# Moving VectorE's row sums and the adaLN gate products to other places of an attention layer

## Chip, cores and metric

The kernel runs on one core of one Trainium2 chip. The metric is the device time of one execution in microseconds (us); the median of the runs counts. TensorE is called PE, VectorE DVE, ScalarE ACT, GpSimd POOL, and SyncE, which only issues DMAs, SP.

## What is computed

A two-layer trunk: layer 0 mixes tokens by gated grouped-query attention, layer 1 by a gated linear recurrence. There are 512 latent tokens and 128 prompt tokens (640 in all), 1024 features, 16 heads of 64 and 4 key heads. Cut to what matters here:

```python
sh, sc, g = split(silu(cond) @ ada_w[i] + ada_b[i], 3)      # per layer; two conditions: latent, prompt
h = x * (1 + sc) + sh
q, k, v, gp = split(h @ attn_w_in, ...)                     # layer 0
q, k = rope(rms_norm(q)), rope(rms_norm(k))                 # the prompt tokens without rope
out = (softmax(q @ k.T / 8) @ v * silu(gp)) @ attn_w_out
x = layer_norm(alpha * x + g * out)
```

Each layer thus needs a shift `sh`, a scale `sc` and a gate `g` of 1024 numbers for each of two conditions. Layer 1 needs its shift and scale only when layer 0 is done, and a gate is needed only in the norm that ends its layer.

## The kernel before

**Products.** An fp32 product is done as three matmuls of split operands: hi times hi, lo times hi, hi times lo. A weight tile of 128x1024 comes by DMA on SP into one of three buffers (`raw`), ACT casts it to the high part (line 240) and DVE subtracts for the low part (line 241, `wlo`). The input projection `attn_w_in` has ten chunks of 256 columns: 0 to 3 are the queries of four heads each, 4 and 5 keys and values, 6 to 9 the gate path.

**The lead-in** (`lead_in`) computes the gate path, 16 half tiles of 24 matmuls (`feat_mms`, lines 349 to 351, out `gps`; ACT applies SiLU). Between them stand the query chunk 0's statistics and its later steps: the scale `rq` by POOL (line 191), normalising `qn` (615), rotary products `u` and `r` (654, 656, 658), ACT's cast (693) and DVE's `qs` (694) as a split, PE's transposes (702), ACT's copy into X (704), which frees the PSUM bank; likewise the keys (`sl`, 667; transposes 676).

**Attention.** After the lead-in the attention of four head chunks runs (`att_gen`): scores (869, 870), row maximum `nm` on DVE (964), exponential `p` on ACT (969), reciprocal `rc` on DVE (974), scaling of `p` on POOL (975), transposes (982) and copies `pts` (874) on ACT and DVE, product `pot` (896), gating into `gs` (901). Beside chunk c-1's attention runs `q_gen` for query chunk c = 1, 2, 3: "beside chunk c" here means beside that projection of query chunk c. `weave` mixes the two by a given share. `split_gs` (1106, 1107, the second on POOL) splits the gated output, and `wo_gen` prepares the output weights; the output projection follows.

**Work without a place of its own.** `q_gen` takes a filler and lets it go a step at fixed points, then drains what is left of it ahead of the last query split. There are two kinds:

- `ada_gen(layer)`: the gate of one layer, four steps of PE products over two weight tiles each (`ada_mms`, line 284, loads of `in_ada_s` on SP), each added to `acc` by DVE (321), then four stores on POOL (325). Layer 0's then loads the gate's broadcast, two DMAs on POOL's queue. It stands beside chunk 2 (layer 0) and chunk 3 (layer 1).
- `ada_cols`: shift and scale of layer 1 by row sums on DVE. Of a 128x1024 weight tile (512 KB, `in_ada_c`) and the broadcast SiLU of each condition, one DVE instruction (line 335, `scalar_tensor_tensor`) multiplies and sums along the row; its product is thrown away into a spill tile. There are 16 tiles, so 32 row sums. Twelve tiles (24 sums) are taken in the lead-in, one tile after each half tile, with two buffers (`adaraw`) loaded by `cols_load` on SP and the spill in a part of `gs` that is not yet in use. Four tiles (8 sums) are the filler `cols_gen` beside chunk 1, from the three `raw` buffers and with a spill tile of `prep` (tag `s2`, two buffers, which the key split `s` uses too).

**What sets the order.** The first half is one scheduled block: a scheduler orders each engine's instructions at build, with the code's order as its start. The order on an engine is then fixed, and an instruction that waits holds what is behind it on that engine. SP's loads keep the order of a list (lines 396 to 402).

Of the kernel before, what the change touches and what calls it, by code (L numbers as in the profile page):

```python
# [11 lines left out]
F32 = mybir.dt.float32  # L12
# [6 lines left out]
P = 128  # L19
D = 1024  # L20
# [13 lines left out]
ALPHA = 4.0 ** 0.25  # L34
HALVES = ((0, 320), (320, 640))
RAW_AHEAD = 2
LEAD = (1, 1)
RAW_START = 8
EARLY = 2
# [9 lines left out]
D_OUT = 5.5  # L49
SLIP = 1.0  # L50
COLS = [(s, ft) for s in range(2) for ft in range(KT)]
COLS_LATE = 4


def view(t, off, dims):
# [72 lines left out]
def drain(gen):  # L128
    for _ in gen:
        pass  # L130
# [3 lines left out]
def hybrid_step(ctx: ExitStack, tc: tile.TileContext, a: dict, o: dict):  # L134
# [176 lines left out]
    def gate_load(layer, eng):  # L311
        for s in range(2):
            eng.dma_start(gate[layer][:, s, :], gated[layer][s:s + 1, :].to_broadcast((P, D)))

    def ada_gen(layer):
        acc = rowp.tile([P, CW], F32, tag="row", name="acc")
        nc.gpsimd.dma_start(acc, a["ada_bias"][layer])
        for i in range(4):
            ps = bank1("adaps")
            ada_mms(ps, layer, i)  # L320
            nc.vector.tensor_tensor(acc, acc, ps[:, :CW], ALU.add)
            yield
        yield
        for q in range(4):
            nc.gpsimd.dma_start(gated[layer][:, q * CW:(q + 1) * CW], acc[32 * q:32 * q + 2, :])
        yield
        if layer == 0:
            gate[0] = gsp.tile([P, 2, D], F32, tag="gate", name="gate0")
            gate_load(0, nc.gpsimd)

    def ada_cols(job, raw, spill):

        s, ft = job
        for c in range(2):
            nc.vector.scalar_tensor_tensor(spill, raw, 1.0, silb[:, c, :], ALU.mult, ALU.mult,
                                           accum_out=shsc[1][:, s, ft, c:c + 1])
        if ft == KT - 1:
            nc.vector.tensor_tensor(shsc[1][:, s], shsc[1][:, s], view(adab, (3 + s) * KT, [[1, KT], [0, 2]]), ALU.add)

    def cols_gen():  # L340
        for job in COLS[len(COLS) - COLS_LATE:]:
            ada_cols(job, take(("ada_c",) + job), prep.tile([P, D], F32, tag="s2", name="spill", bufs=2))
            pump()
            yield

    def feat_mms(ps, w, mt, j, hhi, hlo):
        c, t = slice(mt * P, (mt + 1) * P), slice(*HALVES[j])
# [30 lines left out]
    def ada_pieces(sup):  # L378
        return [("ada_s", sup, k) for k in range(KT)]
# [16 lines left out]
        order.extend(pieces("attn_w_in", c))  # L396
    for c in range(3):
        order.extend(pieces("attn_w_in", c + 1))
        order.extend(ada_pieces(c - 1) if c else [("ada_c",) + job for job in COLS[len(COLS) - COLS_LATE:]])
    order.extend(("attn_w_out", nh, i) for nh, i in PIECES)  # L400
    order.extend(("rec_w_in", h, i) for h in range(RH) for i in range(5))
    order.extend(("rec_w_out", nh, i) for nh, i in OUT1)
# [310 lines left out]
    def q_gen(c, X, fill):  # L713

        w = Weights("attn_w_in", c, (nc.vector, nc.vector), tuple(last_split))
        yield
        if c > 1:
            next(fill)
            yield
        pend = None  # L720
        for tt0, n in UNITS:
            ps = yield from tok_unit(w, tt0, n, "qmm")
            rstd = rms_stat(ps, n)
            r = rope_raw(ps, tt0, n, cosq, sinq, qg)
            yield
            if pend:
                for i in range(pend[1]):
                    pend[0](i)
                    yield
            next(fill, None)  # L730
            yield
            yield
            qn = rms_scale(r, n, rstd)
            yield
# [18 lines left out]
    def lead_in(att):  # L753
# [88 lines left out]

        for _ in range(2):
            cols_load()
        step = 0
        for ch in range(6, 10):
            if ch < 9:
                ws[ch + 1] = Weights("attn_w_in", ch + 1, LEAD_LO)
            w = ws.pop(ch)
            for mt in range(2):  # L850
                for j, (t0, t1) in enumerate(HALVES):
                    ps = bank_any("gps")
                    feat_mms(ps, w, mt, j, hhi, hlo)
                    nc.scalar.activation(gs[:, 2 * (ch - 6) + mt, t0:t1], ps[:, :320], AF.Silu)
                    step += 1
                    if step % 2 or not later:
                        settle()
                    if step % 2 and later:
                        later.pop(0)()
                    if raws:  # L860
                        ada_cols(*raws.popleft(), gs[:, KT - 2:, :].rearrange("p a b -> p (a b)")[:, :D])
                        cols_load()
                    if step > 16 - EARLY:
                        next(att)
        assert not raws


    def score_mms(out, X, c, h, t0, k0, k1):
# [253 lines left out]

    def q_next(c):
        Xs[c] = xq[c % 2].tile([P, 4, NT], F32R, tag="X", name=f"X{c}")
        yield from q_gen(c, Xs[c], ada_gen(c - 2) if c > 1 else cols_gen())

    for c in range(1, 4):
        side.items.append((f"q{c}", q_next(c), lambda c=c: front_of[0] >= c - 1))
# [647 lines left out]
```

## Time and profile before

| | |
|---|---|
| median of 3 runs | 842.29 us (842.24 to 848.55) |
| profiled execution | 844.78 us; its span 843.0 us, mean granted PE clock 0.99 |
| busy, share of the span | PE 808.0 us (96%), DVE 559.9 (66%), ACT 386.5 (46%), POOL 215.8 (26%) |
| DMA | 93.28 MB |
| lead-in's row sums (24) | 71.6 to 122.0 us of the span |
| row sums beside chunk 1 (8) | 144.3 to 185.5 us |

In the trace's rows the first number is the start within the span, the second the duration; then come engine, line, operation, result and operands by the program's names (`out<-in`) and shapes. In brackets stand the engine's idle time ahead of the instruction and what ended it. In a list of waits, "PE x L1 <- DVE y L2: a, n, b" means that PE at line 1 waited for DVE's line 2 for a us in n waits, the longest b. A row of a table of stretches holds the length, and for PE, its weight loads, DVE, ACT and POOL busy time and number of instructions, then the granted clock, the DMA engines' busy share and GB/s. A group's row has three durations in ns: lowest, median, highest.

### The profile page before, as it was taken

The numbers are of one execution on the slowest core, as the hardware profiler recorded it, in microseconds if no ns is written. First come the engines' busy times: TensorE is split into PE (matmuls) and PEld (weight loads), VectorE is DVE, ScalarE is ACT, GpSimd is POOL, SyncE is SP. The second block draws the span as 40 slices with busy tenths as digits, with TensorE's granted clock in tenths as the row PEclk, the third lists the DMA queues.
The fourth block names the chain that finished last, engine by engine and source line by source line (L and its number), as shares of the span: only waits on it lengthen the run. The fifth ranks groups of instructions, "written<-read, shape, count | busy, mean of one in ns | idle before, by whom it ended". The sixth has DMA issues, their size and how long they took to land.

```text
span 843.0 us, 19206 instructions
## 1 busy us (share of the span) xinstructions
PE 808.0 (96%) x8025; PEld 729.2 (87%) x8025; DVE 559.9 (66%) x996; ACT 386.5 (46%) x782; POOL 215.8 (26%) x261
## 2 busy tenths in 40 slices
PE   8999899989999988999999999999999999999994
PEld 6789799878878766888999999999999999998774
DVE  4568882795657674776438575767668575858477
ACT  2252354674656776222434444435434544445232
POOL 0123001443344833010001304143333314121121
PEclk9999899999999999999999999999999999999998
DMA  9944451114151230630322322231322312324041
GB/s 325 397 145 165 151 175 52 51 54 148 51 200 51 101 100 1 225 125 35 108 69 68 103 72 82 83 109 51 107 89 83 99 61 89 120 65 157 23 161 75
DMA packets 34326, 93.28 MB, mean 111 GB/s; under 512 B 5040, under 2 KB 12224, under 8 KB 34240
## 3 DMA queue, kind: packets, MB, share of 16 engines
q1 hardware_dynamic: 23568, 74.10, 25.9%
q0 software_dynamic: 4768, 14.18, 5.4%
q10 hardware_dynamic: 5904, 3.78, 1.5%
q8 instruction: 63, 1.03, 0.5%
q14 instruction: 23, 0.19, 0.1%
HBM read 82.85 MB, written 9.19 MB: 109 GB/s over the span
## 4 chain that ended last, share of the span: by engine, by line
PE 82%; DVE 9%; ACT 2%; DMA 2%; issue 2%; POOL 1%; SPq 0%; DVEq 0%; ACTq 0%; POOLq 0%
PE rps L1319 7%; PE rps L1320 7%; PE rps L1321 7%; PE vgps L1309 5%; PE vgps L1311 5%; PE vgps L1310 5%; PE pot L896 4%; PE outp L1158 4%; PE outp L1160 3%; PE outp L1159 3%; PE pt L982 3%; PE lv L1452 2%; PE acc L536 2%; PE gps L349 2%; PE sc L869 2%
## 5 line engine op out<-in xcount | busy, mean ns | idle before, releaser
L1319 PE MATMUL rps<-h1hi,rhi 128*128 128x320 f32 x368 | 118.4, 322 | 0.0
L1320 PE MATMUL rps<-h1lo,rhi 128*128 128x320 f32 x368 | 113.9, 309 | 0.0
L1321 PE MATMUL rps<-h1hi,rlo 128*128 128x320 f32 x368 | 113.8, 309 | 0.0
L975 POOL TENSOR_SCALAR p<-p,rc 128x640 f32<-128x640 f32 x64 | 58.8, 921 | 116.6 <-DVE rc L974 102.3
L1319 PEld LDWEIGHTS rps<-h1hi,rhi 128*128 128x128 f32 x368 | 69.2, 188 | 1.3
L1320 PEld LDWEIGHTS rps<-h1lo,rhi 128*128 128x128 f32 x368 | 69.3, 188 | 0.0
L1321 PEld LDWEIGHTS rps<-h1hi,rlo 128*128 128x128 f32 x368 | 69.1, 188 | 0.0
L241 DVE TENSOR_TENSOR rlo<-raw,rhi 128x1024 fp32r<-128x1024 f32 x32 | 45.0, 1409 | 33.8 <-ACT rhi L240 33.8
L964 DVE TENSOR_REDUCE nm<-sc 128x1 f32<-128x640 f32 x64 | 52.0, 818 | 23.2 <-PE sc L870 22.8
L1480 POOL COPY At<-near 32x160 f32<-32x160 f32 x32 | 14.0, 438 | 196.8 <-DVE near L1442 195.8
L969 ACT ACTIVATE p<-sc,nm 128x640 f32<-128x640 f32 x64 | 51.2, 802 | 27.2 <-DVE nm L964 19.3
L240 ACT CAST rhi<-raw 128x1024 fp32r<-128x1024 f32 x32 | 33.6, 1049 | 52.0 <-PE rps L1320 48.8
L1430 ACT COPY kc<-A 128x640 f32<-128x640 f32 x40 | 32.2, 806 | 54.4 <-DVE A L1461 50.5
L1309 PE MATMUL vgps<-rhi,h1hi 128*128 128x256 f32 x180 | 51.5, 286 | 0.0
L1310 PE MATMUL vgps<-rlo,h1hi 128*128 128x256 f32 x180 | 50.9, 283 | 0.0
L1311 PE MATMUL vgps<-rhi,h1lo 128*128 128x256 f32 x180 | 50.9, 283 | 0.0
L982 PE MATMUL pt<-small,p 128*128 128x128 f32 x320 | 48.6, 276 | 1.4 <-ACT pts L874 0.9
L869 PE MATMUL sc<-kk,X 128*128 128x320 f32 x128 | 42.6, 343 | 6.1 <-ACT p L969 6.0
L874 ACT COPY pts<-pt 128x512 f32<-128x512 f32 x64 | 35.8, 591 | 24.4 <-PE pt L982 24.1
L982 PEld LDWEIGHTS pt<-small,p 128*128 128x128 f32 x320 | 37.1, 140 | 7.8 <-issue 5.3
L1309 PE MATMUL vgps<-wspare,h1hi 128*128 128x256 f32 x140 | 41.8, 298 | 0.0
L896 PE MATMUL pot<-pts,vv 128*64 128x256 f32 x320 | 38.9, 386 | 2.4 <-DVE pts L874 2.4
(301 smaller groups left out, 2423.6 us busy)
## 6 DMA issues: line engine op xcount, KB each, us to landing
raw<-in_rec_w_in SPq DMA_DIRECT2D x40, 512.0 KB, 3.7
raw<-in_ada_m SPq DMA_DIRECT2D x16, 512.0 KB, 8.0
raw<-in_attn_w_in SPq DMA_DIRECT2D x16, 512.0 KB, 4.2
raw<-in_ada_s SPq DMA_DIRECT2D x16, 512.0 KB, 4.4
adaraw<-in_ada_c SPq DMA_DIRECT2D x12, 512.0 KB, 3.8
raw<-in_attn_w_out SPq DMA_DIRECT2D x8, 512.0 KB, 4.1
raw<-in_rec_w_out SPq DMA_DIRECT2D x8, 512.0 KB, 3.5
x1d<-y SPq DMA_DIRECT2D x5, 512.0 KB, 2.6
```

The source lines that it names most:

```text
L869: nc.tensor.matmul(out, X[:, h, t0:t0 + P], kk[:, c, k0:k1], start=True, stop=False)
L896: nc.tensor.matmul(pot[j * HD:(j + 1) * HD, :CW], vv[:, slot, c * HD:(c + 1) * HD], moving[j], start=first, stop=last)
L964: nc.vector.tensor_reduce(nm[:, 0:1], sc[:, :, :320], AX.XY, ALU.max, negate=True)
L969: return nc.scalar.activation(halves(p[:]), sc[:, :, :320], AF.Exp, bias=nm[:, 0:1], accum_out=su[:, 0:1])
L975: nc.gpsimd.tensor_scalar(p, p, rs[:, 0:1], 1.0, ALU.mult, ALU.mult)
L982: nc.tensor.transpose(pt[:, i * 256 + q * P:i * 256 + (q + 1) * P], ps[q][:, (k0 + i) * P:(k0 + i + 1) * P], ident)
L1309: nc.tensor.matmul(out, h1hi[:, k, t], hi, start=(k == 0), stop=False)
L1310: nc.tensor.matmul(out, h1hi[:, k, t], lo, start=False, stop=False)
L1311: nc.tensor.matmul(out, h1lo[:, k, t], hi, start=False, stop=(k == KT - 1))
L1319: nc.tensor.matmul(ps[:, j, :320], hi[:, k, :], h1hi[:, k, t], start=(k == 0), stop=False)
L1320: nc.tensor.matmul(ps[:, j, :320], hi[:, k, :], h1lo[:, k, t], start=False, stop=False)
L1321: nc.tensor.matmul(ps[:, j, :320], lo[:, k, :], h1hi[:, k, t], start=False, stop=(k == KT - 1))
```

## The change

Four things are changed; the number of row sums, products, loads and stores stays.

1. The lead-in takes eleven tiles (22 row sums) in place of twelve. How many sums follow each half tile is set by the table `ROWS_AT`: none after the first four, one after the fifth and sixth, two after the seventh to the fifteenth, none after the last. Each is "issued after" the SiLU of its half tile (`issue_after` names an instruction that must have been issued before), and what is left is drained at the end.
2. The lead-in's spill tile is the part of `gs` only up to the twelfth half tile, then the `s2` tile of `prep`.
3. The fillers are exchanged: layer 0's gate stands beside chunk 1, layer 1's beside chunk 2, and five tiles (10 row sums) beside chunk 3. The loads of layer 0's gate broadcast move from the end of its products to the end of those five tiles. The list of SP's loads follows.
4. A filler's steps are at spots given by `FILL_AT` ("0b": after the first token tile of unit 0; "0e", "2e", "4e": after units 0, 2, 4), so four steps and the drain, and for row sums a step is one sum.

```diff
+FILL_AT = {1: "0b0e2e4e", 2: "0b0e2e4e", 3: "0b0e2e4e"}
-COLS_LATE = 4
+COLS_LATE = 5
+ROWS_AT = (0, 0, 0, 0, 1, 1, 2, 2, 2, 2, 2, 2, 2, 2, 2, 0)
...
     def ada_gen(layer):
...
-        if layer == 0:
-            gate[0] = gsp.tile([P, 2, D], F32, tag="gate", name="gate0")
-            gate_load(0, nc.gpsimd)
-
-    def ada_cols(job, raw, spill):
+
+    def ada_cols(job, raw, spill, after):
 
         s, ft = job
         for c in range(2):
-            nc.vector.scalar_tensor_tensor(spill, raw, 1.0, silb[:, c, :], ALU.mult, ALU.mult,
-                                           accum_out=shsc[1][:, s, ft, c:c + 1])
+            with tc.issue_after(after()) if after else ExitStack():
+                nc.vector.scalar_tensor_tensor(spill(), raw, 1.0, silb[:, c, :], ALU.mult, ALU.mult,
+                                               accum_out=shsc[1][:, s, ft, c:c + 1])
+            yield
...
+    def spare():
+        return prep.tile([P, D], F32, tag="s2", name="spill", bufs=2)
+
     def cols_gen():
         for job in COLS[len(COLS) - COLS_LATE:]:
-            ada_cols(job, take(("ada_c",) + job), prep.tile([P, D], F32, tag="s2", name="spill", bufs=2))
+            yield from ada_cols(job, take(("ada_c",) + job), spare, None)
             pump()
-            yield
+        gate[0] = gsp.tile([P, 2, D], F32, tag="gate", name="gate0")
+        gate_load(0, nc.gpsimd)
...
-        order.extend(ada_pieces(c - 1) if c else [("ada_c",) + job for job in COLS[len(COLS) - COLS_LATE:]])
+        order.extend(ada_pieces(c) if c < 2 else [("ada_c",) + job for job in COLS[len(COLS) - COLS_LATE:]])
...
-        if c > 1:
-            next(fill)
-            yield
+        spots = {FILL_AT[c][i:i + 2] for i in range(0, len(FILL_AT[c]), 2)}
...
+                if f"{tt0}{'0abcd'[step]}" in spots:
+                    next(fill, None)
+                    yield
...
-            next(fill, None)
-            yield
+            if f"{tt0}e" in spots:
+                next(fill, None)
+                yield
...
+        silus = []
+
+        def spill():
+            return gs[:, KT - 2:, :].rearrange("p a b -> p (a b)")[:, :D] if len(silus) <= 12 else spare()
+
+        def cols_steps():
+            while raws:
+                yield from ada_cols(*raws.popleft(), spill, lambda: silus[-1])
+                cols_load()
+
+        cgen = cols_steps()
...
-                    nc.scalar.activation(gs[:, 2 * (ch - 6) + mt, t0:t1], ps[:, :320], AF.Silu)
+                    silus.append(nc.scalar.activation(gs[:, 2 * (ch - 6) + mt, t0:t1], ps[:, :320], AF.Silu).ins)
...
-                    if raws:
-                        ada_cols(*raws.popleft(), gs[:, KT - 2:, :].rearrange("p a b -> p (a b)")[:, :D])
-                        cols_load()
+                    for _ in range(ROWS_AT[step - 1]):
+                        next(cgen, None)
...
-        assert not raws
+        drain(cgen)
...
-        yield from q_gen(c, Xs[c], ada_gen(c - 2) if c > 1 else cols_gen())
+        yield from q_gen(c, Xs[c], ada_gen(c - 1) if c < 3 else cols_gen())
```

The next rows show what stands on an engine in a row; line numbers shift by 2 to 27 in the changed kernel. First DVE in the lead-in, from the query statistics (190, then 192) to the first query split `qs`, before:

```order
L190 TENSOR_SCALAR rs_t<-ssq 128x20
L335 SCALAR_TENSOR_TENSOR gs,shsc_80<-adaraw,silb 128x1024 x3
L615 TENSOR_TENSOR qn<-pmm,rq 128x512
L335 SCALAR_TENSOR_TENSOR gs,shsc_80<-adaraw,silb 128x1024
L654 TENSOR_TENSOR u<-qn,sinq 128x512
L656 TENSOR_TENSOR r<-qn,cosq 128x512
L335 SCALAR_TENSOR_TENSOR gs,shsc_80<-adaraw,silb 128x1024
L658 TENSOR_TENSOR r<-r,u 128x512
L615 TENSOR_TENSOR qn<-pmm,rq 128x512
L335 SCALAR_TENSOR_TENSOR gs,shsc_80<-adaraw,silb 128x1024
L654 TENSOR_TENSOR u<-qn,sinq 128x512
L694 TENSOR_TENSOR qs_924<-r,qs_924 128x8x64
```

The same place in the changed kernel:

```order
L192 TENSOR_SCALAR rs_t<-ssq 128x20
L335 SCALAR_TENSOR_TENSOR gs,shsc_80<-adaraw,silb 128x1024 x2
L620 TENSOR_TENSOR qn<-pmm,rq 128x512
L659 TENSOR_TENSOR u<-qn,sinq 128x512
L661 TENSOR_TENSOR r<-qn,cosq 128x512
L663 TENSOR_TENSOR r<-r,u 128x512
L699 TENSOR_TENSOR qs_924<-r,qs_924 128x8x64
```

Six row sums stood between the statistics and the split; two are left, both ahead of `qn`, and two more row sums stand ahead of the statistics in both kernels. On SP the loads `adaraw` were two, then four behind the next two weight tiles of `attn_w_in`; now two come behind the next four weight tiles, and seven behind two more, ahead of the gate products' eight.

DVE at the end of the lead-in, before, up to the first row maxima `nm`; `wlo` are chunk 1's weight splits:

```order
L667 TENSOR_TENSOR sl<-kr,s_1340 128x512
L335 SCALAR_TENSOR_TENSOR gs,shsc_80<-adaraw,silb 128x1024 x5
L667 TENSOR_TENSOR sl<-kr,s_1422 128x256
L241 TENSOR_TENSOR wlo<-raw,whi 128x1024
L964 TENSOR_REDUCE nm<-sc 128x1
L241 TENSOR_TENSOR wlo<-raw,whi 128x1024
L964 TENSOR_REDUCE nm<-sc 128x1
```

And in the changed kernel:

```order
L672 TENSOR_TENSOR sl<-kr,s_1317 128x512
L335 SCALAR_TENSOR_TENSOR gs,shsc_80<-adaraw,silb 128x1024 x6
L672 TENSOR_TENSOR sl<-kr,s_1403 128x256
L243 TENSOR_TENSOR wlo<-raw,whi 128x1024
L335 SCALAR_TENSOR_TENSOR spill,shsc_80<-adaraw,silb 128x1024 x2
L339 TENSOR_TENSOR shsc_80<-shsc_80,small 128x16
L335 SCALAR_TENSOR_TENSOR spill,shsc_80<-adaraw,silb 128x1024 x6
L991 TENSOR_REDUCE nm<-sc 128x1
L243 TENSOR_TENSOR wlo<-raw,whi 128x1024
L991 TENSOR_REDUCE nm<-sc 128x1
```

Eight row sums with the `s2` spill now stand between the first weight split and the first maximum.

DVE at the end of chunk 3, before, from the last normalising `qn` through the last query split; `wolo` are the output weights:

```order
L641 TENSOR_TENSOR qn<-r,rstd 128x256
L321 TENSOR_TENSOR acc<-acc,adaps 128x256
L874 COPY pts<-pt 128x256
L964 TENSOR_REDUCE nm<-sc 128x1
L974 RECIPROCAL rc<-su 128x1
L874 COPY pts<-pt 128x256
L694 TENSOR_TENSOR qs_3552<-qn,qs_3552 128x4x64
L964 TENSOR_REDUCE nm<-sc 128x1
L974 RECIPROCAL rc<-su 128x1 x2
L241 TENSOR_TENSOR wolo<-raw,wohi 128x1024
```

And in the changed kernel:

```order
L646 TENSOR_TENSOR qn<-r,rstd 128x256
L335 SCALAR_TENSOR_TENSOR spill,shsc_80<-raw,silb 128x1024
L1001 RECIPROCAL rc<-su 128x1
L901 COPY pts<-pt 128x256
L1001 RECIPROCAL rc<-su 128x1
L991 TENSOR_REDUCE nm<-sc 128x1
L335 SCALAR_TENSOR_TENSOR spill,shsc_80<-raw,silb 128x1024
L699 TENSOR_TENSOR qs_3546<-qn,qs_3546 128x4x64
L991 TENSOR_REDUCE nm<-sc 128x1
L1001 RECIPROCAL rc<-su 128x1
L335 SCALAR_TENSOR_TENSOR spill,shsc_80<-raw,silb 128x1024
L928 TENSOR_TENSOR gs<-pot,gs 128x256
```

Row sums now stand among the row maxima, reciprocals and copies there, and POOL's four gate stores have left this place.

More of the change, by code (lines that the diff above doesn't have):

```diff
@@ L716, in q_gen @@
         yield
-        if c > 1:
-            next(fill)
-            yield
+        spots = {FILL_AT[c][i:i + 2] for i in range(0, len(FILL_AT[c]), 2)}
         pend = None
         for tt0, n in UNITS:
-            ps = yield from tok_unit(w, tt0, n, "qmm")
+            ps = None
+            gen = tok_unit(w, tt0, n, "qmm")
+            step = 0
+            while ps is None:
+                try:
+                    next(gen)
+                except StopIteration as e:
+                    ps = e.value
+                    break
+                step += 1
+                yield
+                if f"{tt0}{'0abcd'[step]}" in spots:
+                    next(fill, None)
+                    yield
             rstd = rms_stat(ps, n)
@@ L729, in q_gen @@
                     yield
-            next(fill, None)
-            yield
+            if f"{tt0}e" in spots:
+                next(fill, None)
+                yield
             yield
```

## Prediction

> **What bounds the kernel now.** I read the page's busy times first, then the chain that ended last, then TensorE's waits stage by stage.
>
> ```profile
> span 843.0 us, 19206 instructions
> PE 808.0 (96%) x8025; PEld 729.2 (87%) x8025; DVE 559.9 (66%) x996; ACT 386.5 (46%) x782; POOL 215.8 (26%) x261
> PEclk9999899999999999999999999999999999999998
> PE 82%; DVE 9%; ACT 2%; DMA 2%; issue 2%; POOL 1%; SPq 0%; DVEq 0%; ACTq 0%; POOLq 0%
> ```
>
> TensorE (PE) is busy 96% of the span and carries 82% of the chain, so an edit off PE pays only where PE waits, or runs slow. The clock digits show one dip, in the fifth slice (84 to 105 us). VectorE (DVE) is 9% of the chain: it is the one that PE waits for. The next three views are PE's waits between 82 and 142 us, stretches of that part (the columns are length, then busy time and instructions per engine, clock, DMA) and DVE just ahead.
>
> ```profile
> PE qps L702 <- DVE qs L694: 3.9, 1, 3.9
> 86.40:90.30 3.90, 0.00 (x1) 0.00 (x1) 3.90 (x9) 1.05 (x2) 0.00 (x0) 0.80 0.23 70
> 91.78:95.64 3.86, 3.86 (x15) 3.86 (x15) 3.86 (x8) 1.57 (x3) 0.00 (x0) 0.51 0.28 113
> 105.00:140.00 35.00, 35.00 (x257) 34.97 (x255) 19.22 (x30) 17.73 (x35) 0.00 (x0) 1.00 0.36 121
> ```
>
> ```profile
> 77.94 4.47 POOL L191 TENSOR_TENSOR rq<-rs_t,mhalf 128x20 f32<-128x20 f32 x1 [7.90 <-DVE rs_t L190]
> 82.45 0.69 DVE L615 TENSOR_TENSOR qn<-pmm,rq 128x512 f32<-128x512 f32 x1 [0.85 <-POOL rq L191]
> 83.06 1.21 DVE L335 SCALAR_TENSOR_TENSOR gs<-adaraw,silb 128x1024 f32<-128x1024 f32 x1
> 84.19 0.69 DVE L654 TENSOR_TENSOR u<-qn,sinq 128x512 f32<-128x512 f32 x1
> 84.80 0.69 DVE L656 TENSOR_TENSOR r<-qn,cosq 128x512 f32<-128x512 f32 x1
> ...
> 87.75 1.22 DVE L335 SCALAR_TENSOR_TENSOR gs<-adaraw,silb 128x1024 f32<-128x1024 f32 x1
> 89.49 0.69 DVE L694 TENSOR_TENSOR qs<-r,qs 128x512 fp32r<-128x512 f32 x1
> ```
>
> Reader, see this: PE stands still for 3.9 us because the first query split `qs` comes only at 89.49. Between the normalised `qn` and `qs` stand three row sums, some 1.2 us each (the first and the last of them are shown). Behind the stall the granted clock is 0.51 for 3.86 us, while the clock digits ahead of it and behind read 9. From 105 to 140 PE has no idle time, with DVE half free and POOL empty.
>
> PE's waits beside the first query chunk (142 to 192 us) and the stretches of the attention follow.
>
> ```profile
> PE sc L869 <- ACT p L969: 2.1, 4, 0.9
> PE adaps L284 <- DMA raw<-in_ada_s: 1.2, 1, 1.2
> 143.00:193.00 50.00, 45.32 (x363) 39.18 (x362) 42.56 (x99) 32.37 (x75) 24.51 (x22) 1.00 0.22 72
> 193.00:240.00 47.00, 46.54 (x404) 38.19 (x402) 29.81 (x65) 26.90 (x61) 18.47 (x21) 1.00 0.28 101
> 240.00:290.00 50.00, 49.66 (x432) 41.95 (x432) 31.82 (x70) 31.91 (x74) 28.56 (x31) 1.00 0.33 113
> 280.00:290.00 10.00, 10.00 (x91) 7.46 (x89) 7.63 (x17) 7.99 (x19) 9.98 (x12) 1.00 0.26 86
> 290.00:300.00 10.00, 7.48 (x54) 5.29 (x50) 7.78 (x11) 7.40 (x15) 3.95 (x4) 1.00 0.30 91
> ```
>
> Beside chunk 1, which holds eight row sums, PE idles 50 - 45.32 = 4.68 us and DVE is busy 42.56 of 50. Beside chunks 2 and 3, which hold the gates' products, PE idles 0.46 and 0.34. After 290 the projections are used up and PE idles again.
>
> **The change, part by part.** Row sums stay 32 (24 and 8 before, 22 and 10 now) and the gates' products stay the same: nothing is removed, only places move.
>
> *The stall.* The order shows that the first four row sums stand where they stood; the tie names a ScalarE instruction and puts no DVE row behind it. What moves the others is SP: their loads now come behind the next projection weights. Four stand ahead of `qn` as before (two ahead of the statistics, two under POOL's 4.47 us), so `qn` stays at 82.45. The three sums between it and `qs`, and the one under the idle before it, are gone. Then `qn`, `u`, `r`, `r` follow at 0.60 (84.80 less 84.19 gives 0.61): the last ends at 82.45 + 3 x 0.60 + 0.69 = 84.94. ScalarE's cast and `qs` add 0.62 and 0.69 and two hand-overs of 0.04:
>
> ```profile
> 87.27 0.62 ACT L693 CAST qs<-r 128x512 fp32r<-128x512 f32 x1 [0.39 <-DVE r L658]
> 86.09 0.31 PE L351 MATMUL gps<-hhi,wlo 128*128 128x320 f32 x1
> 90.33 1.23 PE L702 MATMUL qps<-identr,qs 128*128 128x128 f32 x8 [3.92 <-DVE qs L694]
> 91.78 0.64 PE L349 MATMUL gps<-hhi,whi 128*128 128x320 f32 x1 [0.22 <-ACT X L704]
> 95.64 0.31 PE L351 MATMUL gps<-hhi,wlo 128*128 128x320 f32 x1
> 95.93 0.31 PE L350 MATMUL gps<-hlo,whi 128*128 128x320 f32 x1
> 98.27 0.80 PE L702 MATMUL qps<-identr,qs 128*128 128x128 f32 x8
> ```
>
> So `qs` ends at 86.3, and PE's third half tile at 86.09 + 0.31 = 86.40: the wait is 0 to 0.2. From 86.40 to 95.64 there were 9.24 us. Now: 0.1 of wait; the eight transposes and the copy that frees a bank, 1.2 (between 0.80, eight transposes at full clock, and 1.45, from 90.33 to 91.78 at half clock); and the 14 matmuls that start from 91.78 on and before 95.64, at the pitch behind it, (95.93 - 95.64)/2 = 0.145, or 2.03. That is 3.33, a gain of **5.9** (6.4 at best; 4.9 if `qs` is 1 us later).
>
> *The end of the gate projection.* The late sums wait for loads, each for a buffer that an earlier pair frees; the last two pairs come just ahead of the first maximum and the second weight split of chunk 1.
>
> ```profile
> 137.89 0.82 DVE L964 TENSOR_REDUCE nm<-sc 128x1 f32<-128x640 f32 x1 [12.22 <-PE sc L870]
> 140.03 1.23 DVE L241 TENSOR_TENSOR wlo<-raw,whi 128x1024 fp32r<-128x1024 f32 x1 [1.32 <-ACT whi L240]
> 142.75 0.28 PE L359 MATMUL qmm<-wlo,hhi 128*128 128x256 f32 x1
> adaraw<-in_ada_c SPq DMA_DIRECT2D x12, 512.0 KB, 3.8
> 132.45 0.46 PE L676 MATMUL kps<-identr,s 128*128 128x128 f32 x4
> ```
>
> PE needs that split at 142.75 - 5.9 = 136.9. The spill tile of the fourth last sum waits for the transposes at 132.45, now 126.6, with 0.4 for four: it ends near 128.3. A load of 3.9 and the last pair bring 134.7, then `nm` 0.75 and the split 1.15 (each 0.08 less than its row, as 83.06 is less than 82.45 + 0.69): 136.6. The margin is 0.3, so I take **0.4** lost (0 to 3.2, see the rivals). Ahead of it DVE had 35 - 19.22 = 15.8 us free, which hides the rest of the moved sums, and POOL has none there to disturb.
>
> *Chunk 1.* Eight sums leave (about 8 x 1.22 = 9.8 us of DVE) and the first gate's products come. The nearest rows are 193 to 240 and 240 to 290, which held such products: 0.46 and 0.34 idle. At best 4.2 is won; the least is 1.5, if only the load's 1.2 and a third of a microsecond go. I take **3.2**, since the softmax of the bounds is still there.
>
> *Chunk 2* gets one layer's gate products in place of the other's, the same loads, products and stores: nothing.
>
> *Chunk 3 up to 290.* Four sums come, at half tiles. Without the load's wait, eight cost 3.5 us in chunk 1, so 0.44 each or 1.8 at most, and nothing at least, because 18 of 50 us of DVE are free: **1.0**.
>
> *Its end.* Six sums are drained one after the other, around the last query split, with the loads of the output weights behind them on SP.
>
> ```profile
> 289.17 2.52 DVE L694 TENSOR_TENSOR qs<-qn,qs 128x256 fp32r<-128x256 f32 x1
> 287.71 2.13 POOL L325 DMA_DIRECT2D gated<-acc  x4
> L335 DVE SCALAR_TENSOR_TENSOR gs<-adaraw,silb x24: 1214/1224/1226, 71.6 to 122.0; 128x1024 f32<-128x1024 f32 x24
> L335 DVE SCALAR_TENSOR_TENSOR spill<-raw,silb x8: 1208/1214/1747, 144.3 to 185.5; 128x1024 f32<-128x1024 f32 x8
> ```
>
> They add 6 x 1.22 = 7.3 us. DVE is idle 2.37 + 2.22 = 4.6 between 280 and 300, and the split's 2.52 holds some 2.0 of blocking while POOL issues the gates' stores, which leave this place. So the cover is 6.6, nearly all of the 7.3, but not where each is needed. At chunk 1's 0.44 each they cost 2.6; I take **3.0**, between 0 and 7.3 (no cover at all). The gate's loads, two on POOL's queue, now wait for the last sum; the norm behind the output projection is the first to use them, so they cost nothing. Output weights come later by about a sum or two, beside the tail.
>
> The Trainium skill, on its page "SBUF — State Buffer", "Who interferes with whom", says that a DVE instruction with two SBUF inputs and a GpSimd one that reads SBUF exclude each other for a whole instruction, which speaks against taking sums to where POOL is busiest. The row above is milder: beside POOL the eight sums have a median of 1.214 against 1.224 alone, with one at 1.747. By that rule each of the six could add a whole POOL instruction, which would be the third rival; by the row, 0.5 once.
>
> **The sum.** 844.78 (the profiled execution, its span and 1.78 around it) - 5.9 + 0.4 - 3.2 + 1.0 + 3.0 = 840.1. That execution is 2.5 above the median of 842.29, so the median to expect is 842.29 - 4.7 = **837.6**.
>
> **Rivals.**
> 1. *All of it is free.* The stall gives 6.4, chunk 1 4.2, the chunk 3 sums hide in DVE's 4.6 + 2.0 of free time: 10.6 less, 831.7. For it: PE idles 0.34 between 240 and 290. Against it: DVE was 42.56 of 50 busy beside chunk 1 and PE did wait. Chance 0.14.
> 2. *The late sums overrun.* They become the wait that replaces the one removed. If a load takes 5.4 instead of 3.8, two in a row make the split 3.2 late; PE stops there, and with a second stretch at clock 0.51 pays 1.8 more (3.86 - 2.03): 837.6 + 2.8 + 1.8 = 842.2. For it: a margin of 0.3. Against: the median is 3.8 over twelve loads. Chance 0.14. The Trainium skill, "TensorE: Matmul & The Clock Gate", "HAM oscillation — how this bites in real kernels", puts the edge of such a slow stretch at about 3.4 us of idle; the trace agrees as far as one gap of 3.92 shows it.
> 3. *Slower: POOL and DVE take turns at the end of chunk 3.* Each of the six sums waits for, or holds up, one POOL instruction, the size of this one:
>
> ```profile
> 289.85 1.55 POOL L1107 TENSOR_TENSOR hlo<-gs,hhi 128x640 fp32r<-128x640 f32 x1
> ```
>
> Then 6 x (1.22 + 1.55) - 6.6 = 10.0 takes the place of 3.0, and the time is 844.6. It decides from 7.7 on, where the whole sum reaches zero. For it: POOL is busy 9.98 of 10 between 280 and 290. Against it: the median of the eight sums, and POOL's 3.95 in the ten behind. Chance 0.10.
>
> The forecast itself, 834 to 841.5, has 0.58; 0.04 is left for worse. The range is **832.5 to 844.5**: it leaves out about 0.1 below (most of the first rival) and 0.09 above (half of the third, and the rest). A difference of 1% is about what a measurement of this kernel can tell from no change; faster than 833.9 comes from the first rival, 0.14; slower than 850.7 from the third's far end and the rest, 0.05; within 1%, 0.81.
>
> **What the profile of the changed kernel would show.** The stall: PE's wait for `qs` below 0.5, no 0.51 clock between 85 and 100, and the half tile behind it near 87.7. The end of the projection: the last sum before 135, and no PE wait for `wlo`. Chunk 1: PE idle below 1.5 in its fifty microseconds. The end of chunk 3: sums of 1.2 each, and PE idle between 275 and 300 up by 4 at most. I am wrong if `qs` still comes late, if a sum near the maximum stops PE, or if sums of 2 us or POOL scalings of 2 us stand at the end of chunk 3.

## The result and the profile after

The changed kernel takes 841.91 us (median of 20 runs, 838.95 to 844.47), the kernel before 845.27 (20 runs, 842.09 to 848.55): a ratio of 0.9964 with a 95% interval of 0.995 to 0.9978, or 3.0 us less (1.9 to 4.2). The forecast was 4.7 less. The first three runs of the kernel before, with their median of 842.29, had been low: counted from 845.27 the forecast is 840.6. Of the 4.3 us between the forecast time of 837.6 and 841.91, 3.0 are that low start; the rest is the gain that was forecast too large. Below, a ratio difference of 0.001 is 0.85 us, and intervals of differences are worked out from the two intervals as the root of the sum of squares.

The page of the changed kernel: span, busy times and clock digits.

```profile
span 839.4 us, 19201 instructions
PE 811.3 (97%) x8025; PEld 728.5 (87%) x8025; DVE 562.0 (67%) x996; ACT 386.6 (46%) x782; POOL 215.6 (26%) x261
PEclk9999999999999999999999999999999999999998
```

The dip in the fifth slice is gone. PE's waits between 82 and 142 us, then DVE at the end of the lead-in and the matmul behind it:

```profile
PE qps L707 <- DVE qs L699: 0.5, 1, 0.5
PE qmm L364 <- DVE wlo L243: 0.3, 1, 0.3
```

```profile
84.97 0.69 DVE L699 TENSOR_TENSOR qs<-r,qs 128x512 fp32r<-128x512 f32 x1 [0.69 <-ACT qs L698]
133.59 1.22 DVE L335 SCALAR_TENSOR_TENSOR spill<-adaraw,silb 128x1024 f32<-128x1024 f32 x1
134.74 0.82 DVE L991 TENSOR_REDUCE nm<-sc 128x1 f32<-128x640 f32 x1
135.47 1.22 DVE L243 TENSOR_TENSOR wlo<-raw,whi 128x1024 fp32r<-128x1024 f32 x1
136.75 0.38 PE L364 MATMUL qmm<-wlo,hhi 128*128 128x256 f32 x1 [0.25 <-DVE wlo L243]
```

The first query split starts at 84.97 in place of 89.49, and PE waits 0.5 us for it in place of 3.9. The last row sum of the lead-in ends at 134.8, and the weight split behind it makes PE wait 0.3.

The same stretches as before (length; busy time and instructions of PE, PEld, DVE, ACT, POOL; clock, DMA share, GB/s):

```profile
105.00:140.00 35.00, 34.75 (x258) 34.52 (x257) 23.00 (x38) 17.15 (x36) 1.61 (x2) 1.00 0.47 166
143.00:193.00 50.00, 48.65 (x412) 39.92 (x413) 32.86 (x77) 28.78 (x67) 21.66 (x24) 1.00 0.35 121
193.00:240.00 47.00, 46.61 (x400) 38.83 (x399) 32.52 (x68) 27.59 (x62) 17.44 (x20) 1.00 0.25 91
240.00:290.00 50.00, 47.45 (x372) 40.04 (x371) 39.61 (x79) 33.87 (x77) 29.75 (x27) 1.00 0.11 39
290.00:300.00 10.00, 8.15 (x46) 5.16 (x46) 9.98 (x23) 8.21 (x16) 5.34 (x6) 0.83 0.51 177
283.00:303.00 20.00, 16.91 (x111) 11.81 (x109) 19.67 (x41) 13.39 (x26) 11.54 (x11) 0.91 0.47 161
```

Beside chunk 1 PE's idle time falls from 4.68 to 1.35 us. Beside chunk 3 it rises from 0.34 to 2.55. Between 290 and 300 DVE is full and the granted clock is 0.83. The end of chunk 3 in rows, DVE and then POOL:

```profile
281.36 2.58 DVE L335 SCALAR_TENSOR_TENSOR spill<-raw,silb 128x1024 f32<-128x1024 f32 x1
285.06 1.71 DVE L335 SCALAR_TENSOR_TENSOR spill<-raw,silb 128x1024 f32<-128x1024 f32 x1
286.69 0.41 DVE L699 TENSOR_TENSOR qs<-qn,qs 128x256 fp32r<-128x256 f32 x1
287.83 1.20 DVE L335 SCALAR_TENSOR_TENSOR spill<-raw,silb 128x1024 f32<-128x1024 f32 x1
...
291.25 1.20 DVE L335 SCALAR_TENSOR_TENSOR spill<-raw,silb 128x1024 f32<-128x1024 f32 x1
...
293.52 1.20 DVE L335 SCALAR_TENSOR_TENSOR spill<-raw,silb 128x1024 f32<-128x1024 f32 x1
```

```profile
281.10 1.76 POOL L1134 TENSOR_TENSOR hlo<-gs,hhi 128x640 fp32r<-128x640 f32 x1
288.00 1.70 POOL L1002 TENSOR_SCALAR p<-p,rc 128x640 f32<-128x640 f32 x1 [2.32 <-DVE rc L1001]
291.42 1.70 POOL L1002 TENSOR_SCALAR p<-p,rc 128x640 f32<-128x640 f32 x1 [1.72 <-DVE rc L1001]
293.76 1.62 POOL L1002 TENSOR_SCALAR p<-p,rc 128x640 f32<-128x640 f32 x1 [0.65 <-DVE rc L1001]
```

The row sums stand between DVE's reciprocals, and POOL's scaling of the probabilities waits for those (2.32, 1.72 and 0.65 us). Three of the scalings start just behind a sum and take 1.62 to 1.70 us, where the median of the kernel before is 0.80. PE has no projection left (its last matmul starts at 271.77) and waits behind the scaling, and for a copy that stands behind the longest sum. The longest of its waits between 281 and 300:

```profile
PE pt L1009 <- POOL p L1002: 1.3, 2, 0.9
PE pot L923 <- DVE pts L901: 1.0, 1, 1.0
```

Two neighbouring stretches show what follows:

```profile
292.67:296.08 3.41, 2.15 (x12) 1.50 (x12) 3.41 (x10) 2.21 (x4) 2.76 (x4) 1.00 0.41 160
296.08:299.50 3.42, 3.42 (x19) 1.84 (x18) 3.42 (x5) 3.42 (x8) 1.25 (x2) 0.50 0.85 275
```

PE is busy 2.15 of 3.41 us, and the next 3.42 us run at a clock of 0.50: an estimated 1.7 us more, half of 3.42.

### The profile page after: what moved, and what is told of

The parts are those of the page before. It is cut to its first block, busy times and chain, and to the rows that moved or that the text cites. A ratio compares the mean times of both kernels' runs of the same rounds, so it can differ in the third digit from the quotient of the medians.

```text
span 839.4 us, 19201 instructions
## 1 busy us (share of the span) xinstructions
PE 811.3 (97%) x8025; PEld 728.5 (87%) x8025; DVE 562.0 (67%) x996; ACT 386.6 (46%) x782; POOL 215.6 (26%) x261
## 4 chain that ended last, share of the span: by engine, by line
PE 81%; DVE 10%; ACT 2%; issue 2%; DMA 2%; POOL 2%; SPq 0%; DVEq 0%; ACTq 0%; POOLq 0%
PE rps L1346 7%; PE rps L1347 7%; PE rps L1348 7%; PE vgps L1336 5%; PE vgps L1338 5%; PE vgps L1337 5%; PE pot L923 4%; PE outp L1185 4%; PE outp L1187 3%; PE outp L1186 3%; PE acc L541 3%; PE pt L1009 3%; PE lv L1479 2%; PE sc L896 2%; PE sp L1525 2%
## 5 line engine op out<-in xcount | busy, mean ns | idle before, releaser
L923 PE MATMUL pot<-pts,vv 128*64 128x256 f32 x320 | 40.7, 397 | 1.5 <-DVE pts L901 1.5
```

The costliest lines, as they stand in the source:

```text
L923: nc.tensor.matmul(pot[j * HD:(j + 1) * HD, :CW], vv[:, slot, c * HD:(c + 1) * HD], moving[j], start=first, stop=last)
```

## The experiments

My theory after the result: the lead-in gave what was forecast, chunk 1 also, and the row sums beside chunk 3 took back more than forecast, the six drained ones above all. The main rivals: the lead-in's gain is lost in chunk 1; what costs at the end is the late loading of the output weights; a sum costs its DVE time wherever it stands.

### One part of the change at a time

**The lead-in alone, ten sums beside chunk 1.** The lead-in of the changed kernel, the fillers as before (spots, loads and SP's list go back with them):

```diff
...
-        yield from q_gen(c, Xs[c], ada_gen(c - 1) if c < 3 else cols_gen())
+        yield from q_gen(c, Xs[c], ada_gen(c - 2) if c > 1 else cols_gen())
```

> The lead-in's part of the change alone: 22 row sums at the new places and five late tiles, but the fillers as before (five tiles, ten sums, beside chunk 1, layer 0's gate beside chunk 2, layer 1's beside chunk 3). My theory: the lead-in gives 5.3 us (5.9 in the prediction), and two more sums beside chunk 1 cost 0.44 each: 4.4 us less than before, 840.9 where before is 845.3 (ratio 0.995), so faster than the changed kernel by about 1.4. Rival: what the lead-in gains PE only waits out in chunk 1, since DVE's ten sums and the softmax bound it; then it is within 1.5 us of before (ratio 0.998 or above).

Measured: 843.58 us, ratio 0.9992 (0.9971 to 1.0012). My theory missed by 3.5 us, and the rival's number came. But the trace gives another reason than the rival. PE's longest wait beside chunk 1:

```profile
PE adaps L286 <- DMA raw<-in_ada_s: 3.6, 1, 3.6
```

The stretches there:

```profile
185.00:189.00 4.00, 0.67 (x8) 0.20 (x8) 4.00 (x6) 1.83 (x3) 2.25 (x2) 0.77 0.76 255
189.00:194.00 5.00, 5.00 (x25) 4.65 (x22) 0.84 (x7) 1.37 (x3) 1.60 (x2) 0.50 0.69 245
```

SP's issues of loads (the second number is the time from the first issue of a group to the last):

```profile
172.96 9.85 SPq L221 DMA_DIRECT2D raw<-in_attn_w_in  x2
183.62 6.67 SPq L221 DMA_DIRECT2D raw<-in_ada_s  x4
```

The gate products' first load is issued only at 183.62 (181.22 in the next run), behind the weights of chunk 2, since the row sums hold the three `raw` buffers. PE stands 3.6 us (1.2 before), and a stretch at clock 0.50 follows. (This profiled execution, 847.82, is the slowest of that kernel's twelve, so its sizes are not those of the median.)

**The lead-in alone, eight sums beside chunk 1.** The same with the tiles shared out as before, so 24 sums in the lead-in:

```diff
-COLS_LATE = 5
+COLS_LATE = 4
-ROWS_AT = (0, 0, 0, 0, 1, 1, 2, 2, 2, 2, 2, 2, 2, 2, 2, 0)
+ROWS_AT = (0, 0, 0, 0, 2, 2, 2, 2, 2, 2, 2, 2, 2, 2, 2, 0)
```

> The lead-in's part alone, with the tiles shared out as before: 24 row sums in the lead-in by the new places, eight (four tiles) beside chunk 1 and the gates beside chunks 2 and 3, as before. In the run with ten sums beside chunk 1 the first gate load waited for one of the three weight buffers, which the sums held: PE stood 3.6 us for it near 188, and a half clock of 6.83 us followed. My theory: that wait, not a general bound of chunk 1, ate the lead-in's gain; with eight sums it is 1.2 us again as in the kernel before, and 5 us of the lead-in stay: 840 where before is 845 (ratio 0.994). Rival: chunk 1 is bound by DVE and the softmax, so the gain is lost there whatever the loads do: within 1.5 us of before (ratio 0.998 or above).

Measured: 838.75 us, ratio 0.9932 (0.991 to 0.9954). All of PE's waits from 82 to 190 us:

```profile
PE sc L902 <- ACT p L1002: 2.0, 3, 0.7
PE qps L710 <- DVE qs L702: 0.4, 1, 0.4
PE pt L1015 <- DVE r L633: 0.3, 1, 0.3
```

No wait for a gate load is left, and the lead-in's part alone is worth 5.7 us (3.9 to 7.6), more than the whole change. Two sums more or less beside chunk 1, in a ring of three buffers, made 5.1 us between the two medians (2.5 to 7.6); the wait shown above is of one execution.

**The fillers alone.** The lead-in as before (24 sums), the gates beside chunks 1 and 2, eight sums beside chunk 3:

```diff
-COLS_LATE = 5
+COLS_LATE = 4
...
-                    for _ in range(ROWS_AT[step - 1]):
-                        next(cgen, None)
+                    if raws:
+                        ...
+                        for _ in ada_cols(*raws.popleft(), lambda: sp, None):
+                            pass
+                        cols_load()
```

> The exchange of the fillers alone: the lead-in as before (24 sums), layer 0's gate beside chunk 1, layer 1's beside chunk 2, four tiles (eight sums) beside chunk 3. My theory: chunk 1 gains 2.6 us, chunk 2 loses 0.4, the eight sums cost 0.8 x 4.8 = 3.8: 1.6 us slower than before (ratio 1.002), with PE's wait for the first query split of 3.9 us still there. Rival (the prediction's first rival, all of it is free): 3 to 4 us faster than before (ratio 0.996).

Measured: 844.86 us, ratio 1.0012 (0.9995 to 1.0029). As my theory had it: the exchange as it was made brings nothing, and "all of it is free" falls.

### What the late sums cost

**All ten left out.**

```diff
-            yield from ada_cols(job, take(("ada_c",) + job), spare, None)
+            raw = take(("ada_c",) + job)
+            for c in range(2):
+                nc.vector.tensor_copy(shsc[1][:, job[0], job[1], c:c + 1], raw[:, c:c + 1])
+                yield
...
```

> The changed kernel without its ten late row sums beside chunk 3: each is replaced by a copy of one column (128x1) of the same weight tile, so loads, waits and places stay and the sums' results are left out. My theory: in the changed kernel the ten sums cost what its trace lost between 236 and 333 us against the trace of before, 2.4 us up to the score at 282.5 and 2.4 behind it (1.7 of that a stretch of half clock, 3.41 us long, near 296). Then this kernel is 4 to 5 us faster than the changed one: about 837.5 where before is 845.3 (ratio 0.991), and it shows no clock of 0.5 between 290 and 305. Rival: the loss at the end comes from the output weights that load later, behind the sums' tiles, and not from DVE; then this kernel is within 1.5 us of the changed one, about 841 (ratio 0.995).

Measured: 835.45 us, ratio 0.9895 (0.9868 to 0.9922). The ten sums cost the changed kernel 5.8 us (3.3 to 8.4). The short copies, though, stand at the front of chunk 3 in this kernel's order, between 234.2 and 242.5, so the buffers come free earlier too, and the scheduler orders other instructions anew. In the runs below, too, copies stand that early.

**The six drained ones left out, the four at the spots kept.** 

```diff
+            if n < 2:
+                yield from ada_cols(job, raw, spare, None)
+            else:
+                for c in range(2):
+                    nc.vector.tensor_copy(shsc[1][:, job[0], job[1], c:c + 1], raw[:, c:c + 1])
+                    yield
...
```

> The changed kernel with the four late sums at the spots of chunk 3 kept, and the six drained ones replaced by copies of one column (their results are left out). Without all ten the kernel is 5.8 us faster than the changed one (ratios 0.9895 and 0.9964). My theory: the six drained ones cost the larger part, 4 us (among POOL's work, with DVE full and the half clock behind them), the four at the spots 1.8 (0.44 each, against 1.0 in the prediction): ratio 0.9917. Rival: all ten cost alike, 0.58 each: the six 3.5, and the four 2.3, ratio 0.9923; or the four at the spots cost nothing, ratio 0.9895.

Measured: 836.33 us, ratio 0.9905 (0.988 to 0.993). The six cost 5.0 us (2.6 to 7.4); the four 0.8, which can't be told from nothing. The interval holds all three numbers expected, so this run alone does not say that the six cost more apiece than the four. The traces say where the six cost: in the stretch from the last matmul of the input projection to the first of the output projection, first in the changed kernel, then here:

```profile
271.80:333.20 61.40, 54.51 (x380) 38.49 (x378) 44.92 (x92) 41.69 (x92) 33.55 (x33) 0.97 0.22 78
271.90:328.00 56.10, 52.15 (x379) 37.61 (x377) 36.86 (x80) 41.39 (x92) 29.99 (x31) 1.00 0.16 53
```

The same matmuls take 5.3 us longer with the six sums: PE idles 6.89 us in place of 3.95, and is busy 2.36 longer, with a half clock in it.

**The same, with the buffers held.**

```diff
-                    nc.vector.tensor_copy(shsc[1][:, job[0], job[1], c:c + 1], raw[:, c:c + 1])
+                    nc.vector.tensor_tensor(shsc[1][:, job[0], job[1], c:c + 1], raw[:, c:c + 1], late_qn[0][:, c:c + 1], ALU.mult)
...
```

> The kernel with the four spot sums and without the six drained ones (0.9905), but the six short instructions that stand in for them (results left out) now also read the last normalised query tile, so that they can't run ahead of the place of the drain, and hold the three weight buffers, and the loads of the output weights behind them, until then. My theory: the six sums cost the changed kernel 5 us by their DVE time at that place, and not by the late loads: the ratio stays near 0.9905, 0.993 at most. Rival: the late output weights, whose splits ACT and DVE then do beside the tail, are what costs: the ratio goes to that of the changed kernel, 0.9964, 0.995 at least.

Measured: 837.06 us, ratio 0.9913 (0.9893 to 0.9933). The stand-ins ran from 279.7 to 281.3 of the span, and SP issued the first load of the output weights at 281.16 in place of 242.48. Little of the 5 us came back (0.7, give or take 2.7), so the late loads are not what costs most. But the first low part of the output weights (`wolo`) still came at 287.17, against 287.88 in the run above; in the changed kernel it comes at 296.59, behind the sums. So what the six cost is their DVE time at that place, with the splits that it pushes into the tail; the two are not separated. In all three PE's first output matmul waits 0.5 us for `gs`, and none for the weights.

**The same ten sums, spread.** One table entry of the changed kernel altered:

```diff
-FILL_AT = {1: "0b0e2e4e", 2: "0b0e2e4e", 3: "0b0e2e4e"}
+FILL_AT = {1: "0b0e2e4e", 2: "0b0e2e4e", 3: "0a0b0c0d0e2a2b2c2d2e"}
```

> The changed kernel with one table row altered: the ten late row sums beside chunk 3 get ten spots in its first four token tiles in place of four spots and a drain of six; number, engine and operands are the same. My theory: what costs is that six sums stand at the end of chunk 3, where PE has no projection left to cover DVE; spread ahead of it each costs 0.2 to 0.44 us, ten 2 to 4.4 above the kernel without them (ratio 0.9895), so a ratio of 0.992 to 0.9947 and no half clock near 296. Rival: a sum costs its DVE time beside POOL wherever it stands in chunk 3, so the ratio stays that of the changed kernel, 0.9964 (0.995 or above).

Measured: 834.64 us, ratio 0.9901 (0.988 to 0.9922): 5.3 us (3.2 to 7.5) faster than the changed kernel, and the fastest complete version; that is faster than either number expected. The ten sums (shortest, median, longest in ns; first and last start):

```profile
L335 DVE SCALAR_TENSOR_TENSOR spill<-raw,silb x10: 1198/1213/1782, 232.0 to 260.2; 128x1024 f32<-128x1024 f32 x10
```

The 20 us from 283, as a stretch:

```profile
283.00:303.00 20.00, 16.77 (x124) 13.47 (x126) 16.19 (x30) 17.45 (x40) 11.31 (x13) 1.00 0.33 106
```

The changed kernel's sums run from 235.2 to 293.5; here the last starts at 260.2, while the projection still covers DVE. In the 20 us DVE is busy 16.19 in place of 19.67, PE starts 124 matmuls in place of 111, and the clock is 1.00 in place of 0.91. The ten spots also draw the projection out: its last matmul starts at 277.27 in place of 271.77. So the sums end earlier and the cover ends later.

**Spread spots, sums left out.** The copies for all ten, at the ten spots:

```diff
-FILL_AT = {1: "0b0e2e4e", 2: "0b0e2e4e", 3: "0b0e2e4e"}
+FILL_AT = {1: "0b0e2e4e", 2: "0b0e2e4e", 3: "0a0b0c0d0e2a2b2c2d2e"}
...
+                nc.vector.tensor_copy(shsc[1][:, job[0], job[1], c:c + 1], raw[:, c:c + 1])
...
```

> The kernel with ten spread spots beside chunk 3, but each of the ten sums replaced by a copy of one column (results left out). It tells what the spots alone do from what the sums cost there. My theory: spread sums still cost 0.2 us each, 2 together, so this kernel stands at a ratio of 0.988 to before (the one with the sums at 0.9901), and the ten spots themselves, by drawing the last projection out beside the attention, give 1 us over the kernel with four spots and no sums (0.9895). Rival: spread sums are free and the spots give nothing: 0.9895 to 0.9905.

Measured: 837.21 us, ratio 0.9921 (0.9902 to 0.994). Neither number came: without its sums the spread kernel is no faster than with them. The copies did not stay at the ten spots; the scheduler put them between 235.0 and 242.7. And its profiled execution has a half clock near 290, with no sum near:

```profile
286.65:290.06 3.41, 1.86 (x11) 1.23 (x9) 3.41 (x8) 2.07 (x5) 2.97 (x4) 1.00 0.00 0
290.06:293.47 3.41, 3.18 (x17) 3.01 (x16) 1.21 (x4) 3.10 (x5) 1.79 (x3) 0.50 0.00 0
```

So a half clock there does not need the sums. This kernel and the one with all ten left out do the same work and differ by 2.2 us, give or take 2.8: a rearrangement alone may be worth that much here. Spread sums cost nothing that these runs can tell. Whether the spots themselves help stays open; against the four spots without sums (0.9895) they don't.

### Fewer late sums, more in the lead-in

**Six late, 26 in the lead-in.**

```diff
-COLS_LATE = 5
+COLS_LATE = 3
-ROWS_AT = (0, 0, 0, 0, 1, 1, 2, 2, 2, 2, 2, 2, 2, 2, 2, 0)
+ROWS_AT = (0, 0, 0, 0, 2, 2, 2, 2, 2, 2, 2, 2, 2, 2, 2, 0)
```

> The changed kernel with three late tiles in place of five: 26 row sums in the lead-in, 6 beside chunk 3, of which 2 are drained at its end in place of 6. My theory: the end of chunk 3 gives back 2.5 us or more and the lead-in has DVE time for four more sums (12 of 35 us free between 105 and 140): 5.5 us less than before, 839.8 where before is 845.3 (ratio 0.9935). Rival (the prediction's second, the late sums of the lead-in overrun): two more loads of some 4 us in a queue of two buffers make the second weight split of chunk 1 late by 2 to 4 us, PE waits there, and the time is that of the changed kernel or more (ratio 0.996 to 1.0).

Measured: 840.36 us, ratio 0.9954 (0.9932 to 0.9975): not to be told from the changed kernel, and between the two numbers expected. The rival is partly at work:

```profile
PE qmm L364 <- DVE wlo L243: 1.5, 1, 1.5
```

**Four late, 28 in the lead-in.**

```diff
-COLS_LATE = 5
+COLS_LATE = 2
-ROWS_AT = (0, 0, 0, 0, 1, 1, 2, 2, 2, 2, 2, 2, 2, 2, 2, 0)
+ROWS_AT = (0, 0, 0, 0, 2, 2, 2, 2, 2, 2, 2, 2, 3, 3, 3, 0)
```

> The changed kernel with two late tiles in place of five: 28 row sums in the lead-in, 4 beside chunk 3, all at the spots and none drained. With six late sums the ratio to before was 0.9954. My theory: the end of chunk 3 gives back more, 1 to 2 us, and the lead-in's two last sums stand behind the second weight split, where PE does not wait for them: ratio 0.9935. Rival: the last sums stand between the first maxima of the attention and hold its softmax up by two loads' time, some 3 to 4 us: ratio 0.997 or above.

Measured: 838.66 us, ratio 0.9929 (0.9904 to 0.9954), as my theory had it. But the lead-in shows the prediction's second rival at work. PE's wait:

```profile
PE qmm L364 <- DVE wlo L243: 2.7, 1, 2.7
```

DVE ahead of it:

```profile
134.82 1.22 DVE L335 SCALAR_TENSOR_TENSOR spill<-adaraw,silb 128x1024 f32<-128x1024 f32 x1 [1.23 <-DMA adaraw<-in_ada_c]
137.12 1.22 DVE L243 TENSOR_TENSOR wlo<-raw,whi 128x1024 fp32r<-128x1024 f32 x1
```

The stretch behind it:

```profile
138.10:141.60 3.50, 3.21 (x14) 3.21 (x15) 3.39 (x8) 0.89 (x2) 2.35 (x1) 0.51 0.56 196
```

One pair more, waiting for its load, puts the weight split at 137.12, and PE pays 2.7 us and a stretch of half clock. With 22 sums the wait is 0.3, with 26 it was 1.5.

**Eight late and spread, 24 in the lead-in.** 

```diff
-FILL_AT = {1: "0b0e2e4e", 2: "0b0e2e4e", 3: "0b0e2e4e"}
+FILL_AT = {1: "0b0e2e4e", 2: "0b0e2e4e", 3: "0a0c0d0e2a2c2d2e"}
-COLS_LATE = 5
+COLS_LATE = 4
-ROWS_AT = (0, 0, 0, 0, 1, 1, 2, 2, 2, 2, 2, 2, 2, 2, 2, 0)
+ROWS_AT = (0, 0, 0, 0, 2, 2, 2, 2, 2, 2, 2, 2, 2, 2, 2, 0)
```

> Both lessons joined: 24 row sums in the lead-in (as in the run of the lead-in's part with eight sums, 0.9932, where PE did not wait for the weight split), the gates beside chunks 1 and 2, and the eight late sums spread over the first four token tiles of chunk 3, none drained. My theory: the kernel without late sums stands at 0.9895, eight at 0.2 to 0.44 us add 0.002 to 0.004: 0.9915 to 0.9935, or 838 to 839.5 where before is 845; faster than the changed kernel by 2.5 to 4. Rival: the tighter lead-in makes PE wait for chunk 1's second split again, as with 28 sums (2.7 us and a half clock), and the ratio is 0.995 or above.

Measured: 838.55 us, ratio 0.9941 (0.9919 to 0.9962), a little short of what I expected. PE did not wait for the weight split, so the rival's reason is not it; why this version is 3.4 us behind the one with ten spread sums (1 to 5.9) is not settled. In the two profiles the lead-ins are alike (59.6 and 59.5 us from the first gate matmul to the first score); the difference lies between the first score and the first output matmul, 198.7 against 195.4. It is also 3.9 us (1 to 6.8) behind the kernel without late sums. So spread sums were free in the arrangement of ten, and spreading alone is not shown to be enough.

## Why the prediction was right or wrong

- **The stall, and the lead-in's end:** right. Forecast 5.5 together (5.9 less 0.4); the part alone, with 24 sums in place of 22, measured 5.7, and in the two profiles the time from the first gate matmul to the first score fell from 64.9 to 59.6 us. The split came with a wait of 0.5 (0 to 0.2 forecast) and the margin at the second weight split was as thin as worked out: a wait of 0.3 where 0.4 was taken. The tie to the SiLU did not move the sums: built without it, the changed kernel has the same order on every engine. That it was the loads' place on SP, as the prediction argues, no run isolates.
- **Chunk 1 (and 2):** right, as far as it can be told. Forecast 3.2 and nothing. The kernel without late sums has the lead-in's part (0.9932) and the exchange (0.9895): 3.1 between them, give or take 2.9. PE's idle time there fell by 3.3.
- **Chunk 3 up to 290:** four sums at spots, forecast 1.0, measured 0.8, not to be told from zero.
- **The end of chunk 3:** here the sum failed. The step was the price of the six drained sums: "At chunk 1's 0.44 each they cost 2.6; I take **3.0**". They cost 5.0. The price of chunk 1 was taken for a place with no projection beside it: there a sum ahead of a reciprocal holds up POOL's scaling, the transposes and PE in turn. Counting idle DVE time over twenty microseconds as cover was the error, since each sum needs its gap where it stands. And the sum held no term for the clock: one stretch at 0.50 in the profiled execution, an estimated 1.7 us. Over all runs, one less the granted clock, times the span, is 6.5 us on average for the changed kernel and 4.7 without the six sums: 1.8 apart, give or take 1.1, near the 2 us missed (PE loses it only where it is at work). My sign for this place, PE's idle time between 275 and 300, rose by only 1.1, because PE at half clock counts as busy.
- **A row misread.** The prediction put 2.0 us of the split's 2.52 down to POOL's gate stores. By its rows they end at 289.84, 0.67 into the split; the rest stood under POOL's `hlo`, from 289.85 to 291.40. Without the stores the split takes 0.41, as forecast, but the first sum now meets the `hlo` and takes 2.58.
- **The third rival** (a turn with a POOL instruction for each sum) had the place right, and more of the mechanism than the forecast. Of the six sums two were longer than 1.21, by 1.37 and 0.50; beside three others stood the scalings of 1.70, 1.70 and 1.62, 2.6 above three of 0.80. So five of the six met a turn, 4.5 us in all, half of its 9.3; and a sum above 2 us was one of the prediction's own signs of being wrong. It set this rival aside by the sums' durations alone. Beside two sums of the kernel before, at 159.44 and 173.46, POOL's side shows the turns:

```profile
159.03 2.22 POOL L975 TENSOR_SCALAR p<-p,rc 128x640 f32<-128x640 f32 x1 [1.25 <-DVE rc L974]
173.38 1.87 POOL L975 TENSOR_SCALAR p<-p,rc 128x640 f32<-128x640 f32 x1 [0.78 <-DVE rc L974]
```

But the turns alone are not the cost. Spread, the ten sums met six turns: four sums of 1.58 to 1.78 and scalings of 2.23 and 1.62, 4.2 us in all, and no cost could be told. So it is the place, where no projection covers the chain, that made them count here; the eight spread sums, which fell short, leave open how far that carries.
- **The sum:** with measured terms, 5.7 + 3.1 - 5.8 = 3.0, the 3.0 that was measured. This is no test, since the 3.1 and the 5.8 are themselves differences between the same runs. The bound of 1% that I took for what a measurement can tell was too coarse: twenty runs each told 0.14%.

## What to carry to other kernels

Work that only fills gaps belongs where another engine's long job covers it, spread one instruction at a time: ten sums drained partly at the end of that cover cost 5.8 us, and the same ten, the last of them some 30 us earlier and with the cover drawn out, nothing that could be told (eight spread in another arrangement fell short of that). Price an added instruction by the chain it stands in, not by the engine's idle total. And when two users share a small ring of buffers, look at who loads next: two more users of three buffers took 5 us here, and in the trace PE waited for a load that the edit had not named.

## What the runs showed of the hardware

In these traces the granted clock is 1.00 or 0.50, and a stretch at 0.50 ahead of the end lasts 3.41 us or twice that (6.83 from 88.74 in the kernel before, 3.41 from 296.08 in the changed one). It came after a matmul wait of 2.70 us (28 sums in the lead-in), in the changed kernel after a stretch with no wait above 1.0 us in which PE was busy 2.15 of 3.41, and with the spread sums left out after 1.86 of 3.41. It isn't a matter of busy time alone: in the run of the fillers alone PE was busy for less, and the clock stayed.

```profile
295.60:299.00 3.40, 1.60 (x15) 1.07 (x15) 3.40 (x9) 3.40 (x6) 2.70 (x4) 1.00 0.76 231
299.00:302.40 3.40, 3.40 (x31) 2.72 (x28) 3.40 (x7) 2.02 (x5) 1.36 (x1) 1.00 1.02 358
```

The Trainium skill, "TensorE: Matmul & The Clock Gate", "HAM oscillation — how this bites in real kernels", speaks of some 3.4 us of idle; these runs show the slow stretch after less, and the measurement decides. Part of the spread of single runs goes with the clock: of the 29 runs of the kernel before that stand beside the lead-in alone, the eight below 843 us have a granted clock of 0.992 to 0.994, the six above 847 one of 0.983 to 0.988.

Of the longest sum, 2.58 us from 281.36, the first 1.50 lie under POOL's `hlo`, which ends at 282.86; 1.08 are left behind it, about a sum's own time. The Trainium skill, "SBUF — State Buffer", "Who interferes with whom", has the two exclude each other for a whole instruction, and this row agrees. So do the three long scalings: they start 0.17, 0.17 and 0.24 us behind a sum, and end 0.67, 0.67 and 0.66 behind that sum's end, near the 0.80 that one takes alone.
